# A decoder trunk on one core: GpSimd's arithmetic moved to VectorE and ScalarE

## The chip, the core and the metric
The kernel runs on one core of a Trainium2 chip. The metric is the device time of one execution in microseconds. The engines are called as the profile calls them: PE (TensorE matmuls), PEld (its weight loads), DVE (VectorE), ACT (ScalarE), POOL (GpSimd) and SP (SyncE, which here only issues DMAs).

## The reference
Input x is 1024 x 1024 float32 (tokens by features), batch 1. Two layers follow each other, each with a mixer and an MLP, both post-normed:

```python
for layer in range(2):
    mix = hybrid_mixer(x, ...) if layer % 2 == 0 else recurrent_mixer(x, ...)
    x = layer_norm(DN_ALPHA * x + mix, ln1_g[layer], ln1_b[layer])
    x = layer_norm(DN_ALPHA * x + sqrelu_mlp(x, w1, w2), ln2_g[layer], ln2_b[layer])
```

- `hybrid_mixer` projects x once and feeds two groups of heads. Group A is sliding-window attention: 8 query heads and 2 key heads of width 64, window 128, rotary positions (`x1*cos - x2*sin`, `x2*cos + x1*sin`), softmax with a learned sink per head. Group B is a gated delta rule: 4 heads of width 128; q, k and v pass a causal convolution of four taps and silu, q and k are L2-normalised, and a state is carried over chunks with a per-head decay. One output projection joins both groups.
- `recurrent_mixer` projects to a branch that gets a four-tap convolution, two gates and a linear recurrence along the tokens, and to a gelu gate; then an output projection.
- `sqrelu_mlp` is `relu(x @ w1)**2 @ w2` with 4096 hidden features.

## The kernel before
The 1024 tokens are two chunks of 512, each handled by a generator `stream(c)`: hybrid mixer, MLP, recurrent block, MLP. Chunk 1 follows chunk 0, since it needs its recurrent state, and its work fills the places where chunk 0 waits. Other generators ("mixers": the attention, a head's delta rule, a layernorm) are spawned beside the streams. While the program is built, `Clock` keeps planned times of every operation, with prices by engine, and at each step a loop takes a mixer whose inputs would be ready, or the next piece of a stream. This fixes the order of PE's instructions for good (each depends on the one before it). The order of the other engines' queues is then made by the scheduler. So an operation that is moved to another engine, with another price, can change the order of everything behind it. The loop also chooses, by what has been reached, whether a quarter of an MLP's second product is done `straight` (two eighths, 4 blocks of 48 matmuls in all) or by `seven` products of sums of blocks (7 of 24 matmuls).

Every large product is made of three matmuls in a reduced-precision type: a number x is split into a high part h, a rounded copy, and a low part l = x - h (the remainder), and hi*hi + hi*lo + lo*hi are summed in PSUM (`mm3`). Weights come by `wblock`: SP's queue loads a block of 128x1024 into `ws`, ACT (each fifth time DVE) writes `wh`, and DVE or POOL subtracts to give `wl`. In the hybrid mixer and in the straight part of the MLPs, every second remainder is POOL's; elsewhere `pool=False` gives it to DVE.

POOL also does these: in `conv4` the sum of the first two taps of a head's convolution (the second comes from ACT in a temporary), and DVE adds the last two taps by `scalar_tensor_tensor`; in `attn_prep` the sum of q's two parts (`q_proj` splits q into h and l, into the tiles that later hold attention's output) and in `rope` the product with the cosine; in `attn_block` one of four products of the softmax with 1/denominator, the other three being DVE's; in `head_mid` the product of the mask U with g (tile E), the mask on QK, and the sum of the two parts of z at the end; small copies of three columns between the chunks (`halo`, `rhalo`) and of one (`rlast`). Finally it issues 32 DMAs, which form the sums of weight blocks for `seven` in DRAM.

Space comes in 14 granules of 128x2048 (`gran`, ring "g"), claimed and given back by the generators; `need("g", n)` waits until n are free. `load_x` loads chunk 1's x and needs 4 of them.

Names in the rows: hsc holds the small numbers of a delta-rule head (norms and scales of 128x4 and 128x8), lnw those of a layernorm, asc those of a softmax, S the delta rule's state, angles the cosines and sines, mm and mx PSUM banks, f, s, t rings of 128x512 tiles, g a granule. All engine calls of the helper classes have lines 178 (DVE, ACT, POOL, DMA), 206 (matmul) and 210 (transpose).

Of the kernel before, what the change touches and what calls it, by code (L numbers as in the profile page):

```python
# [17 lines left out]
P = 128  # L18
# [8 lines left out]
MARGIN = 0.5  # L27
WB, WS, HV, LG = 3, 3, 5, 2
RINGS = dict(t=11, s=10, f=4)
# [184 lines left out]
def trunk(ctx: ExitStack, tc, I, out):  # L214
# [127 lines left out]

    def split(h, l, x, key):

        wcount[0] += 1
        (V.tensor_copy if wcount[0] % HV == 0 else S.copy)(h, x)
        (G if key else V).tensor_tensor(l, x, h, ALU.subtract)

    def wblock(src, n=1024, hl=None, pool=True):
# [5 lines left out]
        split(h, l, st, pool and wcount[0] % LG)  # L355
        m = n // 2
        return [h[:, :m], h[:, m:]], [l[:, :m], l[:, m:]]
# [54 lines left out]

    def proj_fm(src, x, bank=None, pool=True):
        wh, wl = wblock(src, pool=pool)
# [8 lines left out]
    def proj_tm(srcs, x, n, nk=KT, pre=None, pool=True):  # L423
        ps = [mm_ps() for _ in range(NT)]
        for k2, src in enumerate(srcs):
            if pre is not None:
                pre(k2)
            wh, wl = wblock(src, 2 * n, pool=pool)
# [100 lines left out]
    def mlp(layer, c, yT, yg, ls, res, tail=False):  # L529
# [58 lines left out]
        def hidden(f, z):  # L588
            ps = yield from proj_fm(w1[f], yT, mm_ps, False)
            used()  # L590
            S.activation(z, ps, AF.Relu)
            S.activation(z, z, AF.Square)
            yield UNIT

        def seven(j, g, done):
# [11 lines left out]
            for i, (a, b, acc, out, sign, last) in enumerate((  # L607
# [16 lines left out]
                for p in range(2):  # L624
# [6 lines left out]
                    V.tensor_tensor(al2, x, ah2, ALU.subtract)  # L631
                    wh, wl = wblock(w2_quarter(layer, j, b)[p * P:(p + 1) * P], pool=False)
                    for k in range(2):
# [15 lines left out]
        def ends():  # L649

            yield from need("g", 5)
            raw = gran()
            blocks = [gran(F32R) for _ in range(4)]
            wb = [wblock(w2_quarter(layer, 3, f"b2{i // 2 + 1}")[i % 2 * P:(i % 2 + 1) * P], pool=False,
                         hl=(t[:, 0:1024], t[:, 1024:2048])) for i, t in enumerate(blocks)]
# [83 lines left out]
    def out_proj(w, oT, resid, yg, ls, res):  # L739
        for n in range(NT):  # L740
            DA.dma_start(ytile(yg, n), resid(n))
        for half in range(2):
            if half == 1:
                res["start"]()
            yield from wait(lambda: kept[0] == 0)
            ps = yield from proj_tm([w[half * 4 + i] for i in range(4)], oT, 512, pool=False)
# [34 lines left out]

    def rope(x, ng, n, a, b):
# [4 lines left out]
        xv = x.rearrange("p g (h d) -> p g h d", d=32)  # L787
        G.tensor_tensor(av, xv, cs, ALU.mult)
        V.tensor_tensor(bv, xv, sn, ALU.mult)
# [30 lines left out]
    def attn_block(c, n, st, oT, tl, o):  # L820
# [84 lines left out]

    def conv4(raw, y, tmp, wt, bias=None, pool=True):
        if bias is None:
            S.activation(y, raw[:, 0:512], AF.Copy, scale=wt(0))
        else:
            S.activation(y, raw[:, 0:512], AF.Identity, bias=bias, scale=wt(0))  # L910
        S.activation(tmp, raw[:, 1:513], AF.Copy, scale=wt(1))
        (G if pool else V).tensor_tensor(y, y, tmp, ALU.add)
        for j in range(2, 4):
            V.scalar_tensor_tensor(y, raw[:, j:j + 512], wt(j), y, ALU.mult, ALU.add)

    def head_front(c, h, x, d, r):
        for j, name in enumerate("kqv"):
# [7 lines left out]
            else:  # L925
                G.tensor_copy(raw[:, 0:3], halo[:, i, :])
            S.copy(raw[:, 3:515], ps)
            if c == 0:
                G.tensor_copy(halo[:, i, :], raw[:, 512:515])
            conv4(raw, y, u, lambda k: W["hcw"][:, i * 4 + k:i * 4 + k + 1])  # L930
            S.activation(u, y, AF.Tanh, scale=0.5)
# [17 lines left out]
    def head_mid(c, h, st, d, oT, r):  # L949
# [170 lines left out]
    def rec_block(c, b, x, hT, s, ring):  # L1120
        xc, xch, xcl = [], [], []
        for j in range(2):
            i = 2 * b + j
            yield from need(ring, 3)
            yield from need("f", 2)
            raw, tmp = tl("f"), ts("f")
            y, h, l = ts(ring), ts(ring, F32R), ts(ring, F32R)
            ps = yield from proj_fm(I["rin"][4 * b + j], x, pool=False)
            if c == 0:
                G.memset(raw[:, 0:3], 0.0)  # L1130
            else:
                G.tensor_copy(raw[:, 0:3], rhalo[:, i, :])
            S.copy(raw[:, 3:515], ps)
            if c == 0:
                G.tensor_copy(rhalo[:, i, :], raw[:, 512:515])
            wt = lambda k: W["rcw"][:, i * 4 + k:i * 4 + k + 1]
            conv4(raw, y, tmp, wt, W["rcb"][:, i:i + 1], False)
            S.copy(h, y)
            V.tensor_tensor(l, y, h, ALU.subtract)
            free("f", raw, tmp)  # L1140
            xc.append(y)
# [5 lines left out]
        for j in range(2):  # L1147
            i = 2 * b + j
            yield from need(ring, 1)
            g2 = ts(ring)  # L1150
            ps = yield from proj_fm(I["rin"][4 * b + 2 + j], x, mx_ps, False)
            S.activation(g2, ps, AF.Square)
# [10 lines left out]
        tt = [ts(ring), ts(ring), ts("f"), ts("f")]  # L1163
        wh, wl = wblock(I["rg"][b], pool=False)
        whv, wlv = ([z.rearrange("p (k c) -> p k c", k=2) for z in w] for w in (wh, wl))
# [27 lines left out]
        for j in range(2):  # L1193
# [31 lines left out]
    def attn_preps(c, st, o):  # L1225
# [23 lines left out]
    def hybrid(c, x, oT, st, rs):  # L1249
# [257 lines left out]
```

## Time and profile before
| | |
|---|---|
| runs, us | 2313.34, 2314.28, 2312.12 (median 2313.34) |
| the profiled execution: its own time, us | 2313.61 |
| its span from the first to the last instruction, us | 2311.8 |
| PE, DVE, ACT, POOL busy, share of the span | 96%, 67%, 44%, 14% |
| mean granted clock of PE | 0.988 |
| DMA, mean GB/s | 142 |

All later times in microseconds are counted from the span's start, in the profiled execution. A group of instructions has its busy time, the mean time of one, and the idle time of its engine just ahead of it with what ended that. Instructions of one engine overlap a little at their ends. The windows of the profile give each engine's busy time in a stretch, so what PE lacks of the stretch's length is time in which it stood.

### The profile page before, as it was taken

How to read it: one execution, taken by the hardware profiler on the slowest of the kernel's cores; microseconds unless marked ns; L12 is line 12 of the kernel's file. 1: busy time of each engine (PE TensorE's matmuls, PEld its weight loads, DVE VectorE, ACT ScalarE, POOL GpSimd, SP SyncE). 2: the span in 40 equal slices, each digit the busy share in tenths (PEclk: the TensorE clock that was granted, in tenths of full speed). 3: DMA queues.
4: the chain of work that ended last, by engine and by line, in shares of the span. 5: the costliest groups of instructions: out<-in, count | busy, mean ns of one | idle time of the engine just before them, and what ended most of it. 6: DMA issues, size and time to landing. Idle time of an engine off the chain costs nothing.

```text
span 2311.8 us, 32057 instructions
## 1 busy us (share of the span) xinstructions
PE 2226.8 (96%) x12460; PEld 1795.1 (78%) x12460; DVE 1552.7 (67%) x2706; ACT 1026.1 (44%) x1759; POOL 313.6 (14%) x248
## 2 busy tenths in 40 slices
PE   8999997999999999999999999989999999999997
PEld 7676776667777888788888878868888887888886
DVE  6788759456645463686666898675565566776477
ACT  5364424433433233454444677474424434444442
POOL 3433223223322120000000001021100000000100
PEclk9999998999999999999999999999999999999999
DMA  4221232556667656677744335222523443454341
GB/s 159 65 74 36 75 123 74 146 153 180 178 177 231 193 162 187 191 237 232 222 139 155 119 129 170 93 74 96 182 95 127 138 146 125 156 166 137 128 159 69
DMA packets 86200, 329.08 MB, mean 142 GB/s; under 512 B 9504, under 2 KB 9888, under 8 KB 77856
## 3 DMA queue, kind: packets, MB, share of 16 engines
q1 hardware_dynamic: 72944, 272.17, 34.4%
q0 software_dynamic: 4608, 33.56, 7.6%
q10 hardware_dynamic: 8496, 21.30, 2.7%
q8 instruction: 98, 1.61, 0.3%
q14 instruction: 54, 0.44, 0.1%
HBM read 318.60 MB, written 75.50 MB: 170 GB/s over the span
## 4 chain that ended last, share of the span: by engine, by line
PE 78%; DVE 13%; ACT 3%; issue 2%; POOL 0%; DMA 0%; DVEq 0%; ACTq 0%; POOLq 0%
PE mm L206 61%; PE mx L206 16%; DVE g L178 5%; DVE t L178 2%; DVE s L178 2%; DVE hsc L178 2%; DVE wl L178 1%; PE mx L210 1%; DVE f L178 1%; ACT wh L178 1%; ACT g L178 1%; ACT t L178 1%; ACT s L178 1%; ACT f L178 0%; ACT L178 0%
## 5 line engine op out<-in xcount | busy, mean ns | idle before, releaser
L206 PE MATMUL mm<-g,wh 128*128 128x512 f32 x2816 | 890.1, 397 | 2.7 <-DVE g L178 2.6
L178 DVE TENSOR_TENSOR wl<-ws,wh 128x1024 fp32r<-128x1024 f32 (+1 forms) x374 | 456.8, 1222 | 340.0 <-ACT wh L178 336.7
L178 ACT CAST wh<-ws 128x1024 fp32r<-128x1024 f32 (+1 forms) x350 | 365.1, 1043 | 719.9 <-PE mm L206 620.6
L206 PEld LDWEIGHTS mm<-g,wh 128*128 128x128 f32 x2816 | 522.2, 189 | 111.3 <-DVE g L178 3.9
L206 PE MATMUL mm<-g,wl 128*128 128x512 f32 x1408 | 551.8, 392 | 0.0
L206 PE MATMUL mm<-wh,s 128*128 128x512 f32 x1152 | 379.8, 395 | 3.6 <-DVE g L178 3.3
L206 PEld LDWEIGHTS mm<-g,wl 128*128 128x128 f32 x1408 | 266.0, 189 | 57.0
L178 POOL TENSOR_TENSOR wl<-ws,wh 128x1024 fp32r<-128x1024 f32 (+1 forms) x64 | 157.2, 2457 | 1010.1 <-ACT wh L178 861.4
L206 PEld LDWEIGHTS mm<-wh,s 128*128 128x128 f32 x1152 | 216.2, 188 | 51.1 <-DVE g L178 3.9
L206 PE MATMUL mm<-wh,g 128*128 128x512 f32 (+1 forms) x768 | 231.4, 379 | 9.3 <-ACT wh L178 6.4
L206 PE MATMUL mm<-wl,s 128*128 128x512 f32 x576 | 224.6, 390 | 0.0
L206 PE MATMUL mx<-wh,s 128*128 128x512 f32 x528 | 172.7, 392 | 1.8 <-DVE s L178 1.8
L206 PEld LDWEIGHTS mm<-wh,g 128*128 128x128 f32 x768 | 142.3, 190 | 35.9 <-ACT wh L178 6.4
L206 PE MATMUL mm<-wl,g 128*128 128x512 f32 (+1 forms) x384 | 143.8, 375 | 0.3 <-DVE wl L178 0.3
L178 ACT CAST s<-g 128x512 fp32r<-128x512 f32 x158 | 96.4, 623 | 100.3 <-PE mm L206 51.2
L178 DVE TENSOR_TENSOR s<-g,s 128x512 fp32r<-128x512 f32 x158 | 106.8, 687 | 38.7 <-ACT s L178 38.5
L206 PEld LDWEIGHTS mm<-wl,s 128*128 128x128 f32 x576 | 108.3, 188 | 20.6 <-DVE wl L178 0.3
L206 PEld LDWEIGHTS mx<-wh,s 128*128 128x128 f32 x528 | 99.1, 188 | 23.2 <-DVE s L178 3.1
L178 DVE CAST wh<-ws 128x1024 fp32r<-128x1024 f32 x88 | 62.7, 712 | 78.1 <-PE mm L206 68.4
L178 DVE TENSOR_TENSOR g<-g,mm 128x512 f32<-128x512 f32 x144 | 95.0, 683 | 20.0 <-PE mm L206 19.5
L206 PE MATMUL mx<-wl,s 128*128 128x512 f32 x264 | 102.8, 389 | 0.0
L206 PEld LDWEIGHTS mm<-wl,g 128*128 128x128 f32 x384 | 73.2, 191 | 12.2 <-DVE wl L178 0.6
(241 smaller groups left out, 2703.2 us busy)
## 6 DMA issues: line engine op xcount, KB each, us to landing
ws<-w SPq DMA_DIRECT2D x234, 512.0 KB, 3.3
ws<-t SPq DMA_DIRECT2D x88, 512.0 KB, 3.3
t<-w POOLq DMA_DIRECT2D x32, 1024.0 KB, 8.6
ws<-hin_fm SPq DMA_DIRECT2D x32, 512.0 KB, 3.3
t<-w SPq DMA_DIRECT2D x16, 1024.0 KB, 7.5
t<-t SPq DMA_DIRECT2D x16, 1024.0 KB, 6.5
ws<-rin SPq DMA_DIRECT2D x32, 512.0 KB, 3.3
ws<-hout SPq DMA_DIRECT2D x16, 512.0 KB, 3.3
```

The lines of the kernel that those rows point to most:

```text
L178: r = f(*a, **k)
L206: ins = self.pe.matmul(out, lhsT, rhs, start=start, stop=stop, skip_group_check=fresh)
L210: return self._pe(self.pe.transpose(out, x, ident), out, [x], 0.00042 * 2 * out.shape[-1])
```

## The change
- `split` gives all weight remainders to DVE; the arguments `key` and `pool` and the constant `LG` go.
- `conv4`: the first tap stays on ACT, the other three are DVE's `scalar_tensor_tensor`; the temporary goes.
- `q_proj` copies q as it is to a granule of its own (`st["qg"]`), freed when the last `attn_prep` is done; `q()` therefore waits for 3 free granules in place of 2. Attention's output tiles are still claimed there (`oT.quad`).
- `rope` takes its source apart from its target and does both products on DVE.
- `attn_block`: all of the softmax scaling is ACT's, one activation for each query head (8 of 128x256 in a block, 128x128 in the first).
- `head_mid`: E is made by four ACT activations with a scale for each; the mask on QK and the sum of z's parts are DVE's.
- The small copies are ACT's. POOL keeps memsets and the DMA issues.

```diff
     def split(h, l, x):
...
-        (G if key else V).tensor_tensor(l, x, h, ALU.subtract)
+        V.tensor_tensor(l, x, h, ALU.subtract)
...
     def q_proj(c, x, st, oT):
         ps = yield from proj_tm([I["hin_q"][i] for i in range(4)], x, 512)
-        st["q"] = [oT.quad(0, n) for n in range(NT)]
+        st["qg"] = gran()
         for n in range(NT):
-            split_ps(*st["q"][n], v4(ps[n]))
+            oT.quad(0, n)
+            S.copy(st["qg"][:, n * CH:(n + 1) * CH], ps[n])
...
-        G.tensor_tensor(av, xv, cs, ALU.mult)
+        V.tensor_tensor(av, xv, cs, ALU.mult)
...
-        G.tensor_tensor(qs, q[0], q[1], ALU.add)
-        rope(kr.unsqueeze(1), 1, n, a[:, :128], b[:, :128])
-        rope(qs, 4, n, a, b)
+        rope(kr.unsqueeze(1), kr.unsqueeze(1), 1, n, a[:, :128], b[:, :128])
+        rope(qs, q, 4, n, a, b)
...
         for m in (0, 2, 1, 3):
-            r = bass_gh(den, m).unsqueeze(2).to_broadcast([P, 2, w])
-            (G if m == 3 else V).tensor_tensor(pm[m][:, :, :w], pm[m][:, :, :w], r, ALU.mult)
+            for g2 in range(2):
+                i = 2 * (2 * (m // 2) + g2) + m % 2
+                S.activation(pm[m][:, g2, :w], pm[m][:, g2, :w], AF.Copy, scale=den[:, i:i + 1])
...
-        S.activation(tmp, raw[:, 1:513], AF.Copy, scale=wt(1))
-        (G if pool else V).tensor_tensor(y, y, tmp, ALU.add)
-        for j in range(2, 4):
+        for j in range(1, 4):
             V.scalar_tensor_tensor(y, raw[:, j:j + 512], wt(j), y, ALU.mult, ALU.add)
...
-                G.tensor_copy(raw[:, 0:3], halo[:, i, :])
+                S.copy(raw[:, 0:3], halo[:, i, :])
...
-        G.tensor_tensor(v4(E), bc_mid(U, 4), bc_last(g, P), ALU.mult)
+        for n in range(NT):
+            S.activation(E[:, n * P:(n + 1) * P], U, AF.Copy, scale=g[:, n:n + 1])
...
-        G.tensor_tensor(v4(QK), v4(QK), bc_mid(U, 4), ALU.mult)
+        V.tensor_tensor(v4(QK), v4(QK), bc_mid(U, 4), ALU.mult)
...
-        G.tensor_tensor(z, oT.h(4 + h), oT.l(4 + h), ALU.add)
+        V.tensor_tensor(z, oT.h(4 + h), oT.l(4 + h), ALU.add)
...
-            yield from need("g", 2)
+            yield from need("g", 3)
             yield from q_proj(c, x, st, oT)
```

How the order moves is shown at three places. The first is DVE's queue at the convolutions of chunk 0's second head (f_..., with the tap weights in sm); before:

```order
L178 SCALAR_TENSOR_TENSOR f_597<-f_596,sm,f_597 128x512 x2
L178 TENSOR_TENSOR wl_892<-ws_889,wh_891 128x1024
L178 SCALAR_TENSOR_TENSOR s_598<-s_598,f_597 128x512
L178 TENSOR_TENSOR s_713<-mx_715,dsc_343 128x512
L178 SCALAR_TENSOR_TENSOR f_654<-f_653,sm,f_654 128x512 x2
L178 SCALAR_TENSOR_TENSOR s_655<-s_655,f_654 128x512
L178 TENSOR_SCALAR hsc_710<-hsc_710 128x8 x2
```

and with the change:

```order
L178 SCALAR_TENSOR_TENSOR f_575<-f_574,sm,f_575 128x512
L178 COPY t_504<-t_503 32x128 x2
L178 SCALAR_TENSOR_TENSOR f_575<-f_574,sm,f_575 128x512
L178 TENSOR_TENSOR wl_874<-ws_871,wh_873 128x1024
L178 TENSOR_TENSOR f_1185<-kraw_309,angles_1183 128x128
L178 TENSOR_TENSOR t_504<-t_504,csb 128x128
L178 SCALAR_TENSOR_TENSOR f_652<-f_651,sm,f_652 128x512
L178 SCALAR_TENSOR_TENSOR s_576<-s_576,f_575 128x512
L178 TENSOR_TENSOR t_504<-t_504,csb 128x128
L178 SCALAR_TENSOR_TENSOR f_652<-f_651,sm,f_652 128x512
L178 STREAM_TRANSPOSE t_504<-t_504 128x128
L178 SCALAR_TENSOR_TENSOR f_652<-f_651,sm,f_652 128x512
```

A convolution has three taps on DVE in place of two, and remainders (wl) stand between them that were POOL's.

The second is SP's queue where chunk 0's heads are loaded (hin_fm) and chunk 1's x (xT) comes in; before:

```order
L178 DMA ws_1168<-hin_fm 128x1024
L178 DMA ws_1306<-hin_fm 128x1024
L178 DMA ws_1467<-hin_fm 128x1024
L178 DMA ws_1484<-xT 128x2x512
L178 DMA ws_1605<-xT 128x2x512
L178 DMA ws_1627<-hin_fm 128x1024
L178 DMA ws_1703<-xT 128x2x512
L178 DMA ws_1731<-hin_fm 128x1024
L178 DMA ws_1782<-xT 128x2x512
```

and with the change, from the same place in the queue:

```order
L178 DMA ws_1154<-hin_fm 128x1024
L178 DMA ws_1376<-hin_fm 128x1024
L178 DMA ws_1451<-hin_fm 128x1024
L178 DMA ws_1628<-hin_fm 128x1024
L178 DMA ws_1709<-hin_fm 128x1024
L178 DMA ws_1764<-hin_fm 128x1024
L178 DMA ws_1957<-hin_fm 128x1024
L178 DMA ws_2007<-xT 128x2x512
L178 DMA ws_2072<-hin_fm 128x1024
L178 DMA ws_2094<-xT 128x2x512
L178 DMA ws_2119<-hin_fm 128x1024
L178 DMA ws_2196<-xT 128x2x512
```

The first load of x stands four weight blocks later.

The third is SP's queue in the first MLP of chunk 0, at its third quarter (w1_0 and w2_0 are weight blocks, t1_0_2 and t2_0_2 sums of them); before:

```order
L178 DMA ws_1091_7840<-w1_0 128x1024
L178 DMA ws_1096_7876<-w1_0 128x1024
L178 DMA ws_1101_7912<-w1_0 128x1024
L178 DMA ws_1106_7949<-w1_0 128x1024
L178 DMA t1_1_1_125<-w2_1 128x2048
L178 DMA ws_1115_7989<-w2_0 128x1024
L178 DMA ws_1118_8020<-w2_0 128x1024
L178 DMA ws_1125_8058<-w2_0 128x1024
L178 DMA ws_1128_8088<-w2_0 128x1024
```

and with the change:

```order
L178 DMA ws_1097_7945<-w2_0 128x1024
L178 DMA ws_1102_7968<-w2_0 128x1024
L178 DMA ws_1105_7988<-w1_0 128x1024
L178 DMA ws_1113_8028<-t1_0_2_113 128x1024
L178 DMA t2_1_0_123<-t1_1_0_121 128x2048
L178 DMA ws_1118_8050<-t1_0_2_113 128x1024
L178 DMA ws_1121_8071<-w1_0 128x1024
L178 DMA ws_1127_8109<-t2_0_2_115 128x1024
L178 DMA ws_1132_8131<-t2_0_2_115 128x1024
L178 DMA ws_1135_8151<-w1_0 128x1024
```

Before, the quarter's blocks of w2 are loaded one after another for `straight`; now the sums of blocks that `seven` takes are loaded between those of w1. Over the whole program PE has 24 matmuls of 128x512 fewer, DVE 6 remainders of weight blocks more than the 64 that it takes over from POOL, and POOL's queue goes from 253 rows to 60.

## Rows read from the trace of the kernel before

**Rows 1.** The page, part 1: busy us (share of the span) xinstructions.
```profile
PE 2226.8 (96%) x12460; PEld 1795.1 (78%) x12460; DVE 1552.7 (67%) x2706; ACT 1026.1 (44%) x1759; POOL 313.6 (14%) x248
```

**Rows 2.** Windows by stage: stretch, length, busy us (xinstructions) by engine, granted clock, DMA share, GB/s.
```profile
0.00:100.00 100.00, 88.80 (x895) 72.94 (x896) 69.03 (x167) 44.89 (x108) 39.14 (x39) 1.00 0.36 119
100.00:200.00 100.00, 88.87 (x621) 65.26 (x621) 88.08 (x215) 52.99 (x154) 38.61 (x36) 0.93 0.21 68
145.00:151.80 6.80, 6.03 (x20) 5.25 (x21) 5.74 (x25) 5.79 (x23) 0.75 (x1) 0.50 0.02 5
200.00:400.00 200.00, 180.17 (x1499) 141.07 (x1497) 147.35 (x373) 79.82 (x198) 49.92 (x37) 0.97 0.24 81
400.00:800.00 400.00, 390.28 (x2890) 298.35 (x2890) 224.99 (x490) 147.39 (x333) 103.88 (x72) 0.99 0.62 178
1000.00:1200.00 200.00, 200.00 (x884) 165.42 (x883) 143.21 (x187) 91.73 (x125) 4.11 (x5) 1.00 0.67 212
```

**Rows 3.** Waits of PE: waiter, released by, us in total, times, longest.
```profile
PE mx L206 <- DVE t L178: 16.3, 8, 7.0
...
PE mm L206 <- ACT wh L178: 6.4, 1, 6.4
```

**Rows 4.** Timelines of DVE, POOL, PE: start, us, instruction [idle before].
```profile
140.07 3.54 DVE L178 TENSOR_SCALAR hsc<-hsc 128x4 f32<-128x4 f32 x2
...
139.98 2.39 POOL L178 TENSOR_TENSOR wl<-ws,wh 128x1024 fp32r<-128x1024 f32 x1
...
145.77 1.22 PE L206 MATMUL mx<-S,s 128*128 128x128 f32 x4 [3.03 <-DVE S L178]
...
273.57 2.52 DVE L178 TENSOR_TENSOR hsc<-hsc 128x4 f32<-128x4 f32 x2
...
273.49 2.38 POOL L178 TENSOR_TENSOR wl<-ws,wh 128x1024 fp32r<-128x1024 f32 x1 [0.38 <-ACT wh L178]
...
375.65 5.71 DVE L178 TENSOR_TENSOR g<-g,s 128x512 f32<-128x512 f32 x4
...
387.69 0.65 PE L206 MATMUL mx<-t 32*32 32x32 f32 x32 [7.00 <-DVE t L178]
```

**Rows 5.** Groups by form, DVE: xcount | busy us, mean ns of one | idle before.
```profile
L178 DVE TENSOR_TENSOR wl<-ws,wh 128x1024 fp32r<-128x1024 f32 x370 | 454.0, 1228 | 339.7 <-ACT wh L178 336.3
...
L178 DVE TENSOR_TENSOR s<-g,s 128x512 fp32r<-128x512 f32 x158 | 106.8, 687 | 38.7 <-ACT s L178 38.5
...
L178 DVE TENSOR_TENSOR g<-g,asc 128x512 f32<-128x512 f32 x21 | 26.1, 1296 | 0.1
...
L178 DVE TENSOR_TENSOR hsc<-hsc 128x4 f32<-128x4 f32 x80 | 24.7, 310 | 3.8 <-ACT t L178 2.2
...
L178 DVE TENSOR_TENSOR f<-f,angles 128x512 f32<-128x512 f32 x8 | 11.8, 1477 | 0.2
...
L178 DVE TENSOR_TENSOR lnw<-lnw 128x2 f32<-128x2 f32 x72 | 10.5, 161 | 0.5
```

**Rows 6.** Groups by form, POOL.
```profile
L178 POOL TENSOR_TENSOR wl<-ws,wh 128x1024 fp32r<-128x1024 f32 x60 | 151.8, 2529 | 963.3 <-ACT wh L178 824.5 <-DVE wh L178 50.8 <-issue 45.3
```

**Rows 7.** Groups by form, ACT.
```profile
L178 ACT ACTIVATE f<-f,sm 128x512 f32<-128x512 f32 x40 | 28.7, 718 | 0.7
...
L178 ACT ACTIVATE g<-g,asc 128x256 f32<-128x256 f32 x56 | 27.6, 495 | 15.6 <-DVE asc L178 15.6
...
L178 ACT ACTIVATE t<-mx,dsc 128x128 f32<-128x128 f32 x22 | 8.1, 367 | 31.4 <-DVE t L178 31.4
```

**Rows 8.** DMA issues: KB each, median us from issue to landing.
```profile
ws<-xT SPq DMA_DIRECT2D x4, 512.0 KB, 3.8
```

More of the change, by code (lines that the diff above doesn't have):

```diff
@@ L27 @@
 MARGIN = 0.5
-WB, WS, HV, LG = 3, 3, 5, 2
+WB, WS, HV = 3, 3, 5
 RINGS = dict(t=11, s=10, f=4)
@@ L341, in trunk, with split, wblock @@
     wcount = [0]
-    def split(h, l, x, key):
+    def split(h, l, x):
         wcount[0] += 1
         (V.tensor_copy if wcount[0] % HV == 0 else S.copy)(h, x)
-        (G if key else V).tensor_tensor(l, x, h, ALU.subtract)
-    def wblock(src, n=1024, hl=None, pool=True):
+        V.tensor_tensor(l, x, h, ALU.subtract)
+    def wblock(src, n=1024, hl=None):
         st = clk.tile("ws", WS, wpool.tile([P, 1024], F32, tag="ws", name=nm("ws"), bufs=WS))[:, :n]
@@ L354, in wblock @@
         h, l = hl
-        split(h, l, st, pool and wcount[0] % LG)
+        split(h, l, st)
         m = n // 2
@@ L411, in load_xT, with proj_fm @@
             V.tensor_tensor(x.l(k), st[j], x.h(k), ALU.subtract)
-    def proj_fm(src, x, bank=None, pool=True):
-        wh, wl = wblock(src, pool=pool)
+    def proj_fm(src, x, bank=None):
+        wh, wl = wblock(src)
         ps = (bank or mm_ps)()
@@ L421, in proj_fm, with proj_tm @@
         return ps
-    def proj_tm(srcs, x, n, nk=KT, pre=None, pool=True):
+    def proj_tm(srcs, x, n, nk=KT, pre=None):
         ps = [mm_ps() for _ in range(NT)]
@@ L427, in proj_tm @@
                 pre(k2)
-            wh, wl = wblock(src, 2 * n, pool=pool)
+            wh, wl = wblock(src, 2 * n)
             for j in range(2):
@@ L588, in hidden @@
         def hidden(f, z):
-            ps = yield from proj_fm(w1[f], yT, mm_ps, False)
+            ps = yield from proj_fm(w1[f], yT, mm_ps)
             used()
@@ L631, in seven @@
                     V.tensor_tensor(al2, x, ah2, ALU.subtract)
-                    wh, wl = wblock(w2_quarter(layer, j, b)[p * P:(p + 1) * P], pool=False)
+                    wh, wl = wblock(w2_quarter(layer, j, b)[p * P:(p + 1) * P])
                     for k in range(2):
@@ L653, in ends @@
             blocks = [gran(F32R) for _ in range(4)]
-            wb = [wblock(w2_quarter(layer, 3, f"b2{i // 2 + 1}")[i % 2 * P:(i % 2 + 1) * P], pool=False,
+            wb = [wblock(w2_quarter(layer, 3, f"b2{i // 2 + 1}")[i % 2 * P:(i % 2 + 1) * P],
                          hl=(t[:, 0:1024], t[:, 1024:2048])) for i, t in enumerate(blocks)]
@@ L745, in out_proj @@
             yield from wait(lambda: kept[0] == 0)
-            ps = yield from proj_tm([w[half * 4 + i] for i in range(4)], oT, 512, pool=False)
+            ps = yield from proj_tm([w[half * 4 + i] for i in range(4)], oT, 512)
             for n in range(NT):
@@ L780, in kv_proj, with rope @@
         yield UNIT
-    def rope(x, ng, n, a, b):
+    def rope(x, src, ng, n, a, b):
         nh = x.shape[2] // 32
@@ L786, in rope @@
         av, bv = (z.rearrange("p (g h d) -> p g h d", g=ng, d=32) for z in (a, b))
-        xv = x.rearrange("p g (h d) -> p g h d", d=32)
-        G.tensor_tensor(av, xv, cs, ALU.mult)
+        xv = src.rearrange("p g (h d) -> p g h d", d=32)
+        V.tensor_tensor(av, xv, cs, ALU.mult)
         V.tensor_tensor(bv, xv, sn, ALU.mult)
@@ L904, in delta_scalars, with conv4 @@
         yield lambda: 0.0
-    def conv4(raw, y, tmp, wt, bias=None, pool=True):
+    def conv4(raw, y, wt, bias=None):
         if bias is None:
@@ L925, in head_front @@
             else:
-                G.tensor_copy(raw[:, 0:3], halo[:, i, :])
+                S.copy(raw[:, 0:3], halo[:, i, :])
             S.copy(raw[:, 3:515], ps)
             if c == 0:
-                G.tensor_copy(halo[:, i, :], raw[:, 512:515])
-            conv4(raw, y, u, lambda k: W["hcw"][:, i * 4 + k:i * 4 + k + 1])
+                S.copy(halo[:, i, :], raw[:, 512:515])
+            conv4(raw, y, lambda k: W["hcw"][:, i * 4 + k:i * 4 + k + 1])
             S.activation(u, y, AF.Tanh, scale=0.5)
@@ L1124, in rec_block @@
             yield from need(ring, 3)
-            yield from need("f", 2)
-            raw, tmp = tl("f"), ts("f")
+            yield from need("f", 1)
+            raw = tl("f")
             y, h, l = ts(ring), ts(ring, F32R), ts(ring, F32R)
-            ps = yield from proj_fm(I["rin"][4 * b + j], x, pool=False)
+            ps = yield from proj_fm(I["rin"][4 * b + j], x)
             if c == 0:
@@ L1131, in rec_block @@
             else:
-                G.tensor_copy(raw[:, 0:3], rhalo[:, i, :])
+                S.copy(raw[:, 0:3], rhalo[:, i, :])
             S.copy(raw[:, 3:515], ps)
             if c == 0:
-                G.tensor_copy(rhalo[:, i, :], raw[:, 512:515])
+                S.copy(rhalo[:, i, :], raw[:, 512:515])
             wt = lambda k: W["rcw"][:, i * 4 + k:i * 4 + k + 1]
-            conv4(raw, y, tmp, wt, W["rcb"][:, i:i + 1], False)
+            conv4(raw, y, wt, W["rcb"][:, i:i + 1])
             S.copy(h, y)
             V.tensor_tensor(l, y, h, ALU.subtract)
-            free("f", raw, tmp)
+            free("f", raw)
             xc.append(y)
@@ L1150, in rec_block @@
             g2 = ts(ring)
-            ps = yield from proj_fm(I["rin"][4 * b + 2 + j], x, mx_ps, False)
+            ps = yield from proj_fm(I["rin"][4 * b + 2 + j], x, mx_ps)
             S.activation(g2, ps, AF.Square)
@@ L1163, in rec_block @@
         tt = [ts(ring), ts(ring), ts("f"), ts("f")]
-        wh, wl = wblock(I["rg"][b], pool=False)
+        wh, wl = wblock(I["rg"][b])
         whv, wlv = ([z.rearrange("p (k c) -> p k c", k=2) for z in w] for w in (wh, wl))
@@ L1200, in rec_block @@
             if c == 0:
-                G.tensor_copy(rlast[:, i:i + 1], hh[:, 511:512])
+                S.copy(rlast[:, i:i + 1], hh[:, 511:512])
             g2 = gate[j]
@@ L1231, in attn_preps @@
             yield from attn_prep(c, n, st, slot["tl"], o[n])
+        free("g", st["qg"])
     def attention(c, st, oT, o):
```

5 lines of the change are left out of this document (1 added, 4 removed).

## The prediction
> **What bounds the kernel now.** I read four views in this order: the page's engine shares, the windows by stage, TensorE's (PE's) waits with the timelines around three of them, and the groups by form.
>
> The shares name PE as the bound: 2226.8 of 2311.8 us busy, against 1552.7 us of VectorE (DVE), 1026.1 us of ScalarE (ACT) and 313.6 us of GpSimd (POOL) [rows 1]. So a change on the other engines pays only through time in which PE stands or runs at half clock. The profiled execution took 2313.61 us, 0.27 us over the median of the three runs (2313.34); the sum is made against 2313.6.
>
> The windows say where that time lies. From 1000 to 1200 us, where POOL does next to nothing, PE is busy for all 200 us and does 884 matmuls, 0.226 us each, at full granted clock. In the first 800 us it stands for 11.2 + 11.1 + 19.8 + 9.7 = 51.8 us, and the granted clock averages 0.93, 0.97 and 0.99 in three of those four windows [rows 2]. In one dip, from 145.0 to 151.8 us, it is 0.50, so 1.2 of 2.4 GHz [rows 2], and PE had stood for 3.03 us just then [rows 4]. A microsecond at half clock loses half a microsecond of work, so the means stand for 0.07 x 100 + 0.03 x 200 + 0.01 x 400 = 17 us lost. Of the 51.8 us, 6.4 us are the wait for the first weights [rows 3] and stay. **What there is to win in the first 800 us is 45.4 + 17 = 62 us.** The same stage holds 39.1 + 38.6 + 49.9 + 103.9 = 231.5 of POOL's 313.6 us [rows 1, 2].
>
> The waits name DVE as the one PE stands behind: their largest group, 16.3 us in 8 waits, is released by it [rows 3]. The timelines say why DVE is late. At 140.07 us two DVE operations on 128x4 numbers last 3.54 us while POOL's weight remainder, begun at 139.98, runs for 2.39; PE then stands 3.03 us for the state S. At 273.57 two more take 2.52 us beside a POOL remainder of 2.38. At 375.65 four layernorm operations take 5.71 us, where 687 ns each would make 2.75, and PE's stand of 7.00 us ends 6.3 us after them [rows 4, 5]. The groups show the same in the mean: two-input operations on 128x4 numbers (hsc) take 310 ns, on 128x2 numbers (lnw), mostly done away from POOL's work, 161; rope's sine product of 128x512 takes 1477 ns, a remainder of that size 687 [rows 5]. So DVE's operations on SBUF tiles are held up while POOL works, some for all of a POOL operation.
>
> **The change part by part.** First DVE's time.
> - Weight remainders: 64 leave POOL, where a full one takes 2529 ns [rows 6], and 6 more come with a regrouping (below). 66 x 1.228 [rows 5] + 4 of half size at 0.6 to 0.7 = 84 us.
> - Convolutions of the heads: 24 POOL adds and 24 ACT taps become 24 DVE taps. At 687 ns, the price of a two-input operation of that size [rows 5], 16.5 us; a tap reads a scalar besides, at a fifth more it is 20; I take 18. In the recurrent layer a tap replaces a DVE add: nothing.
> - Rope's cosine products, the causal mask on QK and the z sum: 24 of 128x512 at 0.687 make 16.5 us, 8 products of a quarter of the size between 1 and 5.5; I take 19.
> - Softmax scaling leaves DVE: 26.1 us [rows 5] and three of half size, together 28. q in one part takes off 8 remainders of 0.687: 5.5 us, and POOL's sum ahead of rope.
> - Regrouping: chunk 0 of the first MLP now does its third quarter by seven products, which brings DVE some 8 us of operand work (14 more remainders of 0.687, 8 fewer of the same size, 4 of twice that size, 2 fewer accumulations).
> - Back from contention: 80 x (0.310 - 0.161) + 8 x (1.477 - 0.687) = 18 us in two groups alone [rows 5]. The ceiling is POOL's whole time, 314 us [rows 1]. I take 80, nearer the rows, because the layernorm operations and many smaller groups show it too.
>
> So DVE gets 84 + 18 + 19 + 8 - 28 - 5.5 = +95 us of work and some 80 back (between 18 and 314). Its load in the first 800 us stays near the present 530 [rows 2], but nothing waits 2.4 us for another engine any more.
>
> ACT gets 64 scalings at the 495 ns of the exponentials of that shape (32 us), 32 decay pieces at 367 ns (12 us) and 48 copies of three columns or one, under 0.37 us each (at most 18 us); it gives 40 taps of 718 ns (29 us) [rows 7]. That is +15 to +33 us on an engine that is 44% busy [rows 1]. I cost it at nothing; if its cover goes, the third rival has the price.
>
> The Trainium skill, Perfetto Trace Analysis, section Optimizing Scalar/DVE Operations, holds against this step that grouped, larger operations give a saturated engine more throughput; the scaling here is cut from 32 operations into 64. The page puts the overhead of one operation on ScalarE at about 93 ns, so by it the 32 extra ones would be an estimated 3 us, if ACT were saturated. At 44% busy the trace does not agree that it is.
>
> PE: seven products take 7 x 24 = 168 matmuls where two eighths done straight take 4 x 48 = 192. 24 x 0.226 [rows 2] = **-5.4 us** on the engine that bounds, the one term that hangs on no wait.
>
> Queues: chunk 1's loads of x move behind four more weight blocks in SP's order, because q's own granule leaves too few free until attention has used it. Projections of chunk 0 hide that, and PE's order up to chunk 1's k and v has the same matmuls; uncovered, four loads in turn at 3.8 us [rows 8] would cost 15 us. POOL's 32 DMA issues stay and no longer queue behind arithmetic. DVE's queue now holds remainders of 1.23 us, so a small operation may stand behind one, where it was held up to 2.4 us by POOL's.
>
> **Sum.** Of the 45.4 us of waits I take 60% as gone (27 us): the three spells I followed all had POOL beside them, but DVE's longer queue will make new ones. Of the 17 us at half clock I take 9, as the dip I followed hangs on such a stand. 2313.6 - 27 - 9 - 5.4 = **2272 us**.
>
> **The rivals.**
> 1. *The waits form anew elsewhere.* PE's order is fixed and DVE's total hardly changes, so other results come late instead. For it: DVE is 147 of 200 us busy from 200 to 400 us. Against it: from 1000 to 1200 us it is as busy (143) and PE never stands [rows 2]. Only -5.4 remains: 2308.
> 2. *DVE becomes the bound, and the kernel slower.* It is busy for 88.1 us from 100 to 200 us and 147 in the next 200 [rows 2]; about a third of the 95 us falls there. If contention gives nothing back, 31 us go straight onto the path: 2313.6 - 5.4 + 31 = 2339. It decides for slower as long as less than 26 of those 31 us come back. Against it: the 3.54, 2.52 and 5.71 us rows [rows 4] have no other cause in sight than POOL.
> 3. *Softmax scaling comes late from ACT.* A block's eight pieces take 8 x 0.495 = 4.0 us in turn, three multiplies on DVE 3 x 0.687 = 2.1 without contention; uncovered that is 1.9 x 8 blocks = 15 us on attention's chain: 2287. The 1296 ns that these multiplies take now [rows 5] make it 3.9 against 4.0, which speaks against it.
>
> **How the numbers follow.** Forecast 0.68, rival 1 0.12, rival 2 0.12, rival 3 0.08. About 0.2% (4.6 us) is what a measurement of this kernel can tell from no change. Rival 1 lies at that edge and is split evenly: faster 0.68 + 0.08 + 0.06 = 0.82, same 0.06, slower 0.12. The range reaches down to nearly all of the 62 us (57) and the 5.4: 2251, and up to rival 1, 2308; rival 2 is left out.
>
> **What would show it.** Right: the hsc group near 160 ns and the sine product near 690; PE's standing in the first 800 us at 25 us or less, the clock there at 0.98 or more; 24 matmuls fewer; no arithmetic on POOL. Wrong: DVE busy for over 95 of 100 us in an early window with PE behind it; PE waiting for ACT's softmax tiles; a stand ahead of chunk 1's first projection; or as much standing as now, released by DVE operations of normal length.

## The result and the profile after

The changed kernel takes **2279.9 us** (2279.06 to 2282.51, 4 runs) against 2313.3: a ratio of **0.986, interval 0.984 to 0.988**. The profiled execution took 2280.57 us, its span is 2278.7; the sum of the prediction ended at 2272.

The page, part 1, answers to [rows 1]:
```profile
PE 2216.7 (97%) x12436; PEld 1790.4 (79%) x12436; DVE 1545.9 (68%) x2809; ACT 1049.1 (46%) x1874; POOL 28.9 (1%) x56
```
PE stands 2278.7 - 2216.7 = 62.0 us instead of 85.0, and its busy time fell by 10.1. DVE has some 95 us more work by the prediction's working and was busy for 7 us less.

The windows by stage, columns as in [rows 2]:
```profile
0.00:100.00 100.00, 91.01 (x931) 73.57 (x932) 72.22 (x194) 44.63 (x117) 0.75 (x10) 1.00 0.35 122
100.00:200.00 100.00, 93.42 (x619) 71.12 (x620) 79.82 (x234) 66.98 (x206) 0.61 (x6) 1.00 0.22 68
200.00:400.00 200.00, 187.89 (x1809) 137.56 (x1809) 132.36 (x423) 94.17 (x278) 0.00 (x0) 0.95 0.19 62
400.00:800.00 400.00, 396.09 (x2658) 316.28 (x2657) 241.06 (x518) 151.21 (x303) 15.41 (x20) 0.99 0.63 183
```
In the first 800 us PE stands for 9.0 + 6.6 + 12.1 + 3.9 = 31.6 us, before 51.8. The granted clock is full (1.00) up to 200 us, but lower than before from 200 to 400 (0.95 against 0.97). By the prediction's way of counting, 0.05 x 200 + 0.01 x 400 = 14 us are still lost to it, where it was 17.

The groups by form answer to [rows 5] and, the last, to [rows 7]; the taps that came to DVE are among them:
```profile
L178 DVE TENSOR_TENSOR wl<-ws,wh 128x1024 fp32r<-128x1024 f32 x436 | 532.6, 1222 | 395.9 <-ACT wh L178 391.8
...
L178 DVE SCALAR_TENSOR_TENSOR f<-f,sm,f 128x512 f32<-128x512 f32 x72 | 53.4, 744 | 6.0 <-ACT f L178 5.3
...
L178 DVE TENSOR_TENSOR hsc<-hsc 128x4 f32<-128x4 f32 x80 | 12.6, 159 | 3.5 <-ACT t L178 1.8 <-ACT s L178 0.3
...
L178 DVE TENSOR_TENSOR lnw<-lnw 128x2 f32<-128x2 f32 x72 | 10.3, 157 | 0.6
...
L178 DVE TENSOR_TENSOR f<-g,angles 128x512 f32<-128x512 f32 x8 | 5.5, 682 | 0.0
...
L178 ACT ACTIVATE g<-g,asc 128x256 f32<-128x256 f32 x112 | 50.7, 497 | 11.6 <-DVE asc L178 11.6
```
The 80 products on 128x4 numbers fell from 310 to 159 ns each; those of the layernorm, which were hardly held up, stay. Rope's sine product (`f<-g,angles`) takes 682 ns instead of 1477. ACT's 112 operations are the 56 exponentials of before and 56 full pieces of the scaling; its whole load grew by 23 us, inside the 15 to 33 of the prediction.

The traces show the contention operation by operation, too. In the kernel before, 78 DVE operations lasted over 60 ns longer than the median of the same form in the changed kernel, and 76 of them overlapped a POOL operation that reads. Of these, 24 are small ones of under 0.2 us that lasted over 1 us, and each of the 24 ended 16 to 31 ns after a POOL operation beside it had ended.

The first spell that the prediction followed [rows 4], in the timelines of DVE and of PE in the changed kernel:
```profile
141.04 0.16 DVE L178 TENSOR_SCALAR hsc<-hsc 128x4 f32<-128x4 f32 x1
141.80 0.16 DVE L178 TENSOR_SCALAR hsc<-hsc 128x4 int32<-128x4 int32 x1
...
150.27 0.61 PE L206 MATMUL mx<-S,s 128*128 128x128 f32 x4
```
Where two such operations lasted 3.54 us beside POOL, each takes 0.16, and the matmul on S has no stand ahead of it.

What is left, in PE's waits, in its timeline from 317 to 347 us, and in the window up to 365 us:
```profile
PE mm L206 <- ACT wh L178: 6.9, 2, 6.4
PE mx L210 <- DVE g L178: 6.2, 4, 2.2
PE mx L206 <- DVE t L178: 5.7, 9, 1.0
```
```profile
318.07 0.45 PE L206 MATMUL mx<-t 32*32 32x32 f32 x32 [0.82 <-DVE t L178]
...
321.39 0.45 PE L206 MATMUL mx<-t 32*32 32x32 f32 x32 [0.97 <-DVE t L178]
...
323.53 1.97 PE L206 MATMUL mx<-g,vraw 128*64 128x512 f32 x2 [1.68 <-DVE g L178]
...
340.91 1.08 PE L206 MATMUL mx<-t,t 64*64 64x64 f32 x8 [2.13 <-DVE asc L178]
...
346.87 1.67 PE L210 MATMUL mx<-csb,g 128*128 128x128 f32 x4 [0.85 <-ACT g L178]
```
```profile
317.00:365.00 48.00, 37.05 (x401) 22.34 (x386) 26.75 (x86) 20.82 (x58) 0.00 (x0) 0.79 0.17 56
```
The wait for DVE's t, which led with 16.3 us [rows 3], is down to 5.7 in nine short ones. From 317 to 365 us PE has only the small chained products of delta rule and attention: it stands for 11.0 of the 48 us, and the granted clock averages 0.79, so some 10 us of the 14 lost to the clock lie here.

### The profile page after: what moved, and what is told of

It is laid out like the page before. It is cut to its first block, busy times and chain, and to the rows that moved or that the text cites. A ratio compares the mean times of both kernels' runs of the same rounds, so it can differ in the third digit from the quotient of the medians.

```text
span 2278.7 us, 31897 instructions
## 1 busy us (share of the span) xinstructions
PE 2216.7 (97%) x12436; PEld 1790.4 (79%) x12436; DVE 1545.9 (68%) x2809; ACT 1049.1 (46%) x1874; POOL 28.9 (1%) x56
## 4 chain that ended last, share of the span: by engine, by line
PE 85%; DVE 9%; ACT 3%; DMA 1%; issue 1%; ACTq 0%; DVEq 0%; SPq 0%
PE mm L206 66%; PE mx L206 17%; DVE g L178 3%; DVE wl L178 2%; PE mx L210 2%; DVE s L178 1%; DMA ws<-w 1%; ACT g L178 1%; ACT wh L178 1%; ACT s L178 1%; DVE t L178 1%; DVE f L178 1%; ACT f L178 0%; ACT t L178 0%; DVE lnw L178 0%
## 5 line engine op out<-in xcount | busy, mean ns | idle before, releaser
L178 DVE TENSOR_TENSOR wl<-ws,wh 128x1024 fp32r<-128x1024 f32 (+1 forms) x444 | 538.3, 1212 | 396.1 <-ACT wh L178 391.8
L178 ACT CAST wh<-ws 128x1024 fp32r<-128x1024 f32 (+1 forms) x356 | 371.5, 1044 | 705.8 <-PE mm L206 605.3
L206 PE MATMUL mm<-wh,g 128*128 128x512 f32 (+1 forms) x768 | 239.3, 383 | 6.6 <-ACT wh L178 6.4
L206 PE MATMUL mx<-wh,s 128*128 128x512 f32 x576 | 187.8, 392 | 1.2 <-DVE s L178 1.2
L178 ACT CAST s<-g 128x512 fp32r<-128x512 f32 x172 | 104.7, 622 | 105.2 <-PE mm L206 53.7
L178 DVE TENSOR_TENSOR s<-g,s 128x512 fp32r<-128x512 f32 x172 | 116.1, 685 | 44.7 <-ACT s L178 44.7
L206 PEld LDWEIGHTS mx<-wh,s 128*128 128x128 f32 x576 | 108.1, 188 | 24.1 <-DVE s L178 2.0
L206 PE MATMUL mx<-wl,s 128*128 128x512 f32 x288 | 112.1, 389 | 0.0
L178 ACT ACTIVATE g<-mm 128x512 f32<-128x512 f32 x100 | 59.3, 593 | 73.0 <-PE mm L206 73.0
```

The lines of the kernel that those rows point to most:

```text
L178: r = f(*a, **k)
L206: ins = self.pe.matmul(out, lhsT, rhs, start=start, stop=stop, skip_group_check=fresh)
```

## The experiments

Each was timed beside the kernel before (2312.7 to 2313.4 us in these comparisons).

**1. The remainders alone.** The kernel before, with every weight remainder on DVE.
```diff
-        split(h, l, st, pool and wcount[0] % LG)
+        split(h, l, st, False)
```


> The kernel before, with the 64 weight remainders moved from POOL to DVE and nothing else (the planner orders anew; no regrouping, so no matmul is saved). Contention theory: POOL's arithmetic falls from some 287 to some 130 us, so about half of DVE's 100 us of hold-ups goes: 2290 to 2304 us, hsc two-input operations between 200 and 260 ns. Rival 'it is the new order and the regrouping': 2306 to 2320, no clear gain. Rival 'DVE becomes the bound': over 2320.

Measured: 2303.55 us, ratio 0.996 (0.994 to 0.997). The time is as the contention theory said, the other sign is not: the 128x4 products still take 300 ns, not 200 to 260, beside POOL's other arithmetic (POOL is busy for 167.5 us in all).

**2. All but the remainders.** The changed kernel, every second remainder of the same blocks back on POOL (50 now, where the kernel before had 64); the regrouping stays. The arguments that choose the blocks come back with it.
```diff
...
-        V.tensor_tensor(l, x, h, ALU.subtract)
+        (G if key else V).tensor_tensor(l, x, h, ALU.subtract)
...
```


> The changed kernel with the weight remainders back on POOL in the places of before (convolution, rope, masks, softmax stay moved; 24 matmuls fewer, as in the change). Contention theory: POOL keeps some 157 us of the longest operations, the ones of 2.4 us, so half of the gain stays away: 2290 to 2302 us, hsc between 200 and 260 ns. Rival 'order and regrouping': about the changed kernel's 2280.

Measured: 2294.43 us, 0.992 (0.990 to 0.993); 128x4 products 221 ns, both as the contention theory said. The two halves give 9 and 18 us, some 28 of the 33. The planner makes an order of its own for each of them, so this is no exact sum; but neither part carries the change alone, and DVE's products stay slower as long as POOL keeps some of its arithmetic.

**3 and 4. POOL reads, or only writes, beside the changed kernel.** The changed kernel with the order of every instruction on PE, DVE and ACT as it was; at 50 of the weight blocks whose remainders were POOL's in the kernel before (64 there), POOL does work that nobody uses. In the third it reads:
```diff
...
         V.tensor_tensor(l, x, h, ALU.subtract)
+        if key:
+            for i in range(3):
+                nc.gpsimd.tensor_tensor(dum, h[:, :256], h[:, 256:512], ALU.subtract)
...
```


> The changed kernel, with the orders of PE, DVE and ACT left as they are, plus POOL arithmetic that nobody needs: where POOL had a remainder before, it now subtracts 128x256 pieces of the high part from each other, three times, into a tile that nothing reads. No engine waits for its result. Contention theory: the hold-ups of DVE come back without any changed order and without POOL on any chain: hsc at 200 ns or more, 2286 to 2300 us. Rival 'only POOL's slowness on the chain counted' and rival 'order': 2279 to 2283, as the changed kernel.

In the fourth it only writes, six fills of dum (128x256) at each place. A dependency that is added by hand (left out below) holds them back until h is there.
```diff
...
+        if key:
+            m = nc.gpsimd.memset(dum, 0.0)
+            for _ in range(5):
+                nc.gpsimd.memset(dum, 0.0)
...
```


> As the run before, but POOL only writes: six memsets of 128x256 float32 in the same places, held back until the high part is written, so that POOL works at the same times without reading. Orders of PE, DVE and ACT as in the changed kernel. If it is POOL's reading that holds up DVE's operations of two SBUF inputs, nothing happens: 2279 to 2284 us, hsc near 160 ns. If any use of SBUF by POOL holds DVE up, or the waits themselves cost, it lies with the run before.

Measured: **2292.71 us** where POOL reads (0.991, 0.990 to 0.993), **2280.43** where it writes (0.986, 0.985 to 0.988). Groups by form, POOL and DVE, of the kernel whose POOL reads:
```profile
L351 POOL TENSOR_TENSOR dum<-wh 128x256 fp32r<-128x256 f32 x150 | 172.8, 1152 | 1308.3 <-ACT wh L178 645.8 <-DVE wh L178 627.5 <-DVE asc L178 12.3
...
L178 DVE SCALAR_TENSOR_TENSOR f<-f,sm,f 128x512 f32<-128x512 f32 x72 | 58.1, 811 | 5.9 <-ACT f L178 5.3
...
L178 DVE TENSOR_TENSOR hsc<-hsc 128x4 f32<-128x4 f32 x80 | 14.8, 187 | 3.4 <-ACT t L178 1.8 <-ACT s L178 0.2
```
And of the kernel whose POOL writes:
```profile
L352 POOL MEMSET dum<- 128x256 f32 x250 | 78.6, 315 | 14.2
...
L178 DVE SCALAR_TENSOR_TENSOR f<-f,sm,f 128x512 f32<-128x512 f32 x72 | 53.4, 745 | 6.0 <-ACT f L178 5.3
...
L178 DVE TENSOR_TENSOR hsc<-hsc 128x4 f32<-128x4 f32 x80 | 12.7, 160 | 3.5 <-ACT t L178 1.8 <-ACT s L178 0.3
...
L178 DVE TENSOR_SCALAR kc<-kc 128x8 f32<-128x8 f32 x2 | 0.7, 326 | 0.0
```
Reading for 172.8 us on POOL makes DVE busy for 25 us more than writing does (1572.9 against 1547.6 us) and the kernel 12 us slower, although the 128x4 products rise only to 187 ns, short of the 200 that were expected. One other thing moved: ACT's casts waited 3.5 us in all until POOL had read an older wh. It doesn't carry the difference: PE's wait for ACT's wh is 6.4 us, all of it the first weights, and between the profiled executions of the changed kernel and of this one, which lie 8 us apart, PE's waits that DVE ends grew from 35.7 to 42.8 us, those that ACT ends from 13.6 to 14.0.

The 94 us of writing leave the time and the two-input groups as they were. Ten one-input DVE operations beside a fill were held for a moment all the same: the two on kc above take 326 ns instead of 169, and in all eight TENSOR_SCALAR, a cast and a copy lost 1.6 us.

The Trainium skill, SBUF — State Buffer, section Who interferes with whom, says that a DVE instruction with two inputs in SBUF contends with a GpSimd instruction that reads SBUF, and not with one that only writes it. The two runs agree.

So the contention is shown by itself, and what costs time is POOL's reading. Its share of the 33 us is not shown. The kernel before had 313.6 - 28.9 = 285 us of POOL arithmetic; scaled by POOL's time, 12.3 x 285 / 173 makes an estimated 20 us. Scaled by the time that DVE loses (27 us in this run against the changed kernel, some 102 in the kernel before, see below), it would be 46, more than the whole gain.

One rival has no run of its own: that POOL's slower operations stood on the path themselves. Rows of the kernel before leave little room for it: PE never waits for POOL, its weight loads do once for 2.7 us, ACT once for 3.4 and DVE for 5.9 us in all, and POOL has 0% of the chain that ended last:
```profile
DVE f L178 <- POOL f L178: 5.9, 6, 1.9
ACT wh L178 <- POOL wl L178: 3.4, 1, 3.4
PEld mx L206 <- POOL f L178: 2.7, 1, 2.7
```

**5. No regrouping.** Chunk 0's first MLP does six eighths straight.
```diff
-        while e < 8 and not (...
+        while e < (6 if layer == 0 and c == 0 else 0) or e < 8 and not (...
```


> The changed kernel, but chunk 0 of the first MLP does six eighths straight before the seven products, as the kernel before did. 24 matmuls more than the change. If the regrouping is worth what its matmuls cost (24 x 0.226 us): 2284 to 2288 us. If the gain of the change was mainly the new grouping: 2300 or more. If regrouping cost as much on DVE as it saved: 2278 to 2282.

Measured: 2286.31 us, 0.988 (0.987 to 0.990): 6.4 over the changed kernel for 24 matmuls more, where the sum had 5.4. It is PE's busy time that grew (2223.1 against 2216.7 us), not its standing.

**6. Softmax scaling on DVE.**
```diff
-                S.activation(..., AF.Copy, scale=den[:, i:i + 1])
+                V.tensor_scalar(..., den[:, i:i + 1], None, ALU.mult)
```


> The changed kernel with the softmax scaling as tensor_scalar on DVE (64 pieces) in place of ACT. If ACT's pieces hold up attention's chain (the third rival): faster by 4 to 15 us, 2265 to 2276. If ACT had room for them, as the forecast says: 2278 to 2286.

Measured: 2281.53 us, 0.987 (0.985 to 0.988). The same, within what can be told apart, though the planner's order differs from the 1075th matmul on: ACT had the room, and once POOL is silent DVE would have had it too.

**7. Remainders left out.** Some of the remainders that POOL used to do are not computed, and the third product of those blocks reads a tile of zeros; the planner still books the time, so PE's order is that of the changed kernel. The trace has 416 remainders in place of 444, so 28 are left out, not 31.
```diff
...
+        if key:
+            clk.issue("V", [l], [x, h], 0.07 + 1.04e-3 * x.shape[1])
+            skip.add(l.name)
+        else:
             V.tensor_tensor(l, x, h, ALU.subtract)
...
```


> The changed kernel without the subtraction of 31 of the remainders that it took from POOL: the third matmul of those blocks reads a fixed zero tile (this part of the product is left out). The planner still books the time, so PE's order stays. DVE has 31 x 1.22 = 38 us less in the first 800 us. If what is left of PE's standing comes from DVE's longer queue, as the forecast's 60% assumed: PE stands 6 to 12 us less in the first 800 us and the time is 2264 to 2275. If the rest comes from chains that do not queue behind remainders: 2277 to 2282.

Measured: 2282.34 us, 0.986 (0.985 to 0.988), 0.3 over the range of the second theory, with DVE busy for 1515.4 us, 31 less. PE stands 28.8 us in the first 800, 2.9 less and not 6 to 12. The stretch with the largest standing is much as it was (windows, 200 to 400 us):
```profile
200.00:400.00 200.00, 189.31 (x1807) 139.02 (x1806) 130.22 (x420) 93.52 (x275) 0.00 (x0) 0.93 0.19 62
```
So the standing that is left hardly hangs on how much DVE has to do.

**8 and 9. Weight casts between ACT and DVE.** `HV`, every fifth cast on DVE, set to none and to every third.
```diff
-WB, WS, HV = 3, 3, 5
+WB, WS, HV = 3, 3, 100000
```


> The changed kernel with all high parts of weights written by ACT, also each fifth that DVE wrote (88 casts of 0.686 us go, on ACT 1.05 us each: DVE -60 us, ACT +92 us over the whole program). If DVE's load sets the rest of the standing: 2266 to 2276. If ACT's longer cast or its queue then holds weights back: 2282 to 2300.

> The changed kernel, but every third instead of every fifth cast of a weight block is done on VectorE: some 60 casts of about 0.69 us move there from ScalarE, where one takes 1.05; nothing else is set, and the matmuls are as many. With all casts on ScalarE the time rose by 28 us. Theory 'what PE still waits for stands behind casts in ScalarE's queue': 2268 to 2276 us, TensorE standing for 20 us or less in the first 800 us after the first weights. Rival 'VectorE's queue length does not matter either way, as when 38 us of remainders were left out, and the 28 us came of another order of the matmuls': 2277 to 2285 us. Rival 'VectorE, 80 of 100 us busy from 100 to 200 us, becomes the bound there': over 2286 us, with over 90 busy in that window.

Measured: all on ACT **2307.79** us, 0.998 (28 us over the changed kernel; it also lost the regrouping); every third on DVE **2290.81**, 0.991 (11 us over). Both directions lose. The first lies over both of its ranges. The second lies over all that its first two theories allowed; its third doesn't hold either, as DVE is 81.9 us busy from 100 to 200 us, not over 90. Both lose much of it in the same stretch; the windows, of the run with all on ACT and of the other:
```profile
200.00:400.00 200.00, 178.56 (x1745) 132.10 (x1743) 124.47 (x394) 97.98 (x280) 0.00 (x0) 0.92 0.19 61
```
```profile
200.00:400.00 200.00, 180.12 (x1775) 132.37 (x1776) 124.21 (x399) 91.85 (x267) 0.00 (x0) 0.95 0.19 61
```
PE stands there for 21.4 and 19.9 us instead of 12.1. The planner makes a new order from either setting, so the runs compare that order together with the casts; they say nothing of the queue of ACT by itself.

**10 to 12. The granule that q holds.** While the changed kernel is planned, chunk 0's `mix_out` waits for a second free granule as long as chunk 1's q holds one, and 72 products of chunk 1's projection come ahead of the 192 of chunk 0's output projection; the stretch with small products alone follows. The tenth run gives chunk 1's q back its two parts in oT's tiles; the output projection then stands ahead again.
```diff
...
-            S.copy(st["qg"][:, n * CH:(n + 1) * CH], ps[n])
+            if c == 0:
+                S.copy(st["qg"][:, n * CH:(n + 1) * CH], ps[n])
+            else:
+                split_ps(*st["q"][n], v4(ps[n]))
...
```


> The changed kernel, but chunk 1 keeps q in two rounded parts in oT's tiles and adds them on VectorE ahead of the rotation; chunk 0 keeps its own granule. The first MLP of chunk 0 then takes no quarter by seven products up to its sixth eighth, so that there are 24 matmuls of 128x512 more than in the changed kernel, as in the run without the regrouping (2286.3 us); that run is what it is compared with. Theory 'the granule that chunk 1's q holds keeps chunk 0's output projection behind 72 products of chunk 1, and leaves TensorE only chained small products from about 319 to 350 us': TensorE's standing in 200 to 400 us falls from 12.1 to under 6 us, the granted clock there rises from 0.95 to 0.97 or more, and the time is 2268 to 2278 us. Rival 'those waits belong to chunk 0's attention and come wherever it stands': 2283 to 2290 us, with 10 us or more of standing in the same stretch.

Measured: 2284.48 us, 0.988 (0.986 to 0.989), against the fifth run's 0.988 (0.987 to 0.990): no difference, and PE stands for 16.6 us from 200 to 400 us. So this theory falls and its rival holds. The small waits from 317 to 350 are gone, and one large one stands at 360 us (windows, then PE's and DVE's timelines):
```profile
200.00:400.00 200.00, 183.41 (x1661) 141.22 (x1659) 140.61 (x403) 79.06 (x202) 0.94 (x1) 0.96 0.27 85
400.00:800.00 400.00, 398.66 (x2818) 311.54 (x2818) 229.04 (x504) 166.47 (x380) 15.74 (x21) 1.00 0.64 185
```
```profile
369.46 0.65 PE L206 MATMUL mx<-t 32*32 32x32 f32 x32 [9.32 <-DVE asc L178]
```
```profile
357.54 3.10 DVE L178 TENSOR_TENSOR g<-g,s 128x512 f32<-128x512 f32 x5
...
360.55 0.29 DVE L178 TENSOR_TENSOR t<-t,csb 128x128 f32<-128x128 f32 x1
...
361.35 0.16 DVE L178 SCALAR_TENSOR_TENSOR asc<-asc,kc 128x8 f32<-128x8 f32 x1
...
366.29 0.28 DVE L178 TENSOR_TENSOR t<-t,csb 128x128 f32<-128x128 f32 x1
...
367.10 0.16 DVE L178 TENSOR_TENSOR asc<-sm,asc 128x8 f32<-128x8 f32 x1
...
369.10 0.30 DVE L178 STREAM_TRANSPOSE t<-t 128x128 f32<-128x128 f32 x1
```
This wait is the third spell of the prediction: the same 32x32 matmuls, behind the same layernorm products, that stood for 7.00 us in the kernel before [rows 4]. Here those products take 0.62 us each, POOL does no arithmetic, and PE stands longer: the operations on t, which these matmuls read, and the softmax's small ones (asc, which the profile names as the last to end) sit between layernorm products and convolution taps in DVE's queue, each of normal length.

In the eleventh run chunk 0's third quarter is done by seven products besides, without looking at where chunk 1 stands. The edit of the tenth run stays.
```diff
...
-        while e < 8 and not ((c == 1 or sts[1]...
+        while e < 8 and not ((c == 1 or e == 4 or sts[1]...
...
```


> As the run before, and the third quarter of chunk 0's first MLP taken by seven products without looking at where chunk 1 stands, so that the matmuls are as many as in the changed kernel. If the 24 matmuls cost what they did there and there is no new wait, it lies 5 to 6.5 us under the run before; theory 'granule': 2262 to 2273 us, faster than the changed kernel; rival: 2278 to 2284 us. If the stretch of the first MLP was in need of its six straight eighths as cover for chunk 1's layer-1 mixer, new waits show in 400 to 800 us and it is no faster than the run before.

Measured: 2296.77 us, 0.993 (0.991 to 0.994), 12 over the tenth run with 24 matmuls fewer, and over both theories. The wait at 360 us stays, and new ones come, as the expectation's last sentence allowed: 4 us more of standing from 400 to 800 us. The longest of the new ones stands further on than expected, at 909 us (PE's timeline):
```profile
914.91 1.11 PE L210 MATMUL mx<-csb,g 128*128 128x128 f32 x4 [5.71 <-DVE g L178]
```
In the twelfth q of both chunks is in two parts.
```diff
...
-            S.copy(st["qg"][:, n * CH:(n + 1) * CH], ps[n])
+            split_ps(*st["q"][n], v4(ps[n]))
...
```


> The changed kernel with q of both chunks in two parts in oT's tiles, no granule for q at all; 24 matmuls of 128x512 more than in the changed kernel, as in the run without the regrouping (2286.3 us), and one more VectorE addition per tile of q than in the run with chunk 1 alone. Here chunk 0's output projection still stands behind the 72 products of chunk 1's projection in TensorE's order. Theory 'granule' in the form 'what costs is that order, which leaves small products alone': 2281 to 2290 us, with TensorE standing 9 us or more in 200 to 400 us. Rival 'what costs is the granule itself, by a transfer or a tile that waits for it': as the run with chunk 1 alone, within 4 us.

Measured: 2316.75 us, 1.001 (1.000 to 1.002), far over both theories: the planner takes a worse order altogether (clock 0.95 from 100 to 200 us, 14.7 us of standing from 400 to 800). No version was faster than the changed kernel.

## Why the prediction was right, point by point

- **The bound and the mechanism** hold. Most of the time was won where PE stood behind DVE: the waits of PE that DVE ends fell from 62.5 to 35.7 us. Runs 3 and 4 show with the order held fast that POOL's reading makes such waits. Of the signs that were named for it these came: 159 and 682 ns, 24 matmuls fewer, no arithmetic on POOL. Two did not come in full: PE stands for 31.6 us in the first 800, not 25 or less (25.2 after the first weights), and the clock stayed under 0.98 from 200 to 400 us.
- **The sum, term by term**, over the whole span: standing -23.0 (of it -20.2 in the first 800 us) where it had -27; PE's busy time -10.1, of which -5.4 are put down to the 24 matmuls (run 5 gives 6.4) and the other -4.7 to the clock, where it had -9; the windows make the clock's part 17 - 14 = 3 us. Together -33.1 of the -41.4 forecast. **What failed is the size of the two terms for waits and clock.** They took 60% of 45.4 and half of 17 on the ground that "the three spells I followed all had POOL beside them". For the third of them that was no proof: four products that took 5.71 instead of 2.75 us explain 3 of the 7.00 us, and run 10 has 9.32 us there without any POOL arithmetic. And 9 of 17 for the clock had one dip as its ground, which is gone (1.00 from 100 to 200 us); another came from 317 to 365 us.
- **Why 40% would stay** was put wrongly. "DVE's longer queue will make new ones": run 7 took 31 us from DVE and gained nothing. The largest piece of what stays, 11 of the 25.2 us of standing and most of what the clock still costs, is a stretch with small chained products alone. That the planner's order decides where PE stands fits run 10, where this stretch is gone and one long stand has taken its place; runs 8 to 12 all lie 5 to 37 us over the changed kernel, but each has another order in many places at once.
- **DVE's time**: 66 remainders and the 24 taps came as worked out (1222 and 744 ns). 95 of work and the 7 by which DVE's busy time fell make some 102 us given back, where 80 was taken between 18 and 314. The rows bear it out: the 78 operations counted above lasted 84 us too long, and the softmax products and the sine product, whose forms are gone, add an estimated 13 and 6. Rival 2, with DVE as the bound, falls: from 100 to 200 us it is 79.8 us busy, where it was 88.1.
- **ACT costed at nothing** holds: the pieces take 497 ns as taken, PE waits 1.1 us in all for ACT's g, and run 6 finds no gain in having the scaling on DVE, so rival 3 falls. PE's waits that ACT ends did grow, from 9.6 to 13.6 us, mostly for other tiles. By the Trainium skill's rule on larger operations (Perfetto Trace Analysis, Optimizing Scalar/DVE Operations) the finer cut matters on a saturated engine; run 6 shows no price on this one at 46%.
- **Queues costed at nothing**: ACT's casts of chunk 1's later x wait 0.86 and 1.03 us for their loads, and the longest stand of PE from 100 to 200 us is 2.04 us, ended by a temporary of DVE. q's granule does move 72 products of chunk 1 ahead, which the prediction hadn't seen, but run 10 finds no gain in undoing that.
- **Rival 1**, the waits forming anew elsewhere, describes the part that wasn't won, not the result.

**Still open**: whether there is an order without such a stretch. No run holds the order of the changed kernel and takes that stretch away alone.

## What to carry to other kernels

Work that is moved to an idle GpSimd isn't free when it reads SBUF: look for VectorE operations whose mean is far over that of their size, and count what they hold up, not GpSimd's busy share. In a kernel whose order comes from a planner, a change that only moves work also draws a new order, which can cost as much as the change itself wins (here up to 37 us); test the mechanism with the order held fast, as runs 3, 4 and 7 do, before believing a difference. A stand beside a suspect isn't yet caused by it: subtract what the suspect's rows explain, and leave the rest out of the sum.

## What was not expected of the hardware

That DVE operations with one input are held too, and for as long as POOL's operation lasts: the two on 128x4 numbers that took 3.54 us [rows 4] are TENSOR_SCALAR of 0.16 us each in the changed kernel. The first lasted 2.32 us and ended 24 ns after POOL's remainder, the second 1.19 us and ended 26 ns after the POOL operation behind it. And that POOL's writing is cheap, but not without effect: 300 fills of 315 ns left DVE's two-input groups within 4 ns, while eight TENSOR_SCALAR beside them took 273 to 395 ns instead of 165 to 172.
